# Both fixed passes of an expert stage from one dispatch, in a two-layer trunk kernel

## The chip, the core and the metric

The kernel runs on one core of one Trainium2 chip. The metric is the device time of one execution in microseconds. Engines are named as in the profile: PE is the matrix engine (TensorE) and PEld its weight loads, DVE the vector engine, ACT the scalar engine, POOL is GpSimd, and SP (SyncE) issues all transfers from DRAM in one queue. SBUF and PSUM are the on-chip memories; PSUM has eight banks, which the code calls bank(0) to bank(7).

## What is computed

The reference is a trunk of two layers over 512 tokens of width 1024, in float32. Layer 0 mixes tokens with an mLSTM of 4 heads, layer 1 with a short gated convolution; behind each stands a mixture of 32 experts, of which a token uses two. Before each sub-layer stands an RMSNorm with shift, scale and gate from a vector c. Cut to what matters:

```python
for i in range(DEPTH):                      # 2 layers
    h = rmsnorm(x, g) * (1.0 + scale) + shift
    y = mlstm_mixer(h, ...) if i == 0 else short_conv_mixer(h, ...)
    x = x + gate * y
    h = rmsnorm(x, g2) * (1.0 + scale2) + shift2
    # top group of 4, the top 2 of its 8 experts for each token, softmax weights
    out[t] = sum over t's two experts e of w * ((silu(h @ w_gate[e]) * (h @ w_up[e])) @ w_down[e])
    x = x + gate2 * out
return rmsnorm(x, final_g)
```

The mLSTM's head computes decayed scores of queries and keys over the causal triangle, their product with the values, and divides by a normaliser and by the root mean square of the result.

## The kernel before

The tokens lie in four tiles of 128 (TT = 4), a row of 1024 in eight blocks (KT = 8). The order of each engine's instructions is the order in which the program issues them; every engine works its queue in that order. A mixer is a list of steps in which products, small vector work and the adaLN vectors of later sub-layers (ada_third) are woven together by weave; how many of the latter stand where is set by FILL0 and FILL1.

**The ring.** Weights stream through tiles of 1 MB in pools L (2), A (8), B (8) and E (2). Ring.pump issues loads in one fixed order, and a load waits until its pool's oldest tile has been given back by done. The mixer borrows all eight B tiles (mixer_open): h and z in parts (own[0:4]), the split weights, scratch and a gate row. last_chunk gives the first of them back after two products and the second after four, open_ring all eight at the end of the mixer.

**An expert stage.** The 32 experts are worked in 13 passes of two or three experts, each pass with 128 slots for tokens. Passes 0 and 1 (FIXED = 2) hold known experts, so that their weights can be loaded before the routing is known. In a pass, dispatch gathers the tokens of its slots by products with a 0/1 matrix, up_project makes gate and up products, activate applies SiLU on ACT and multiplies on DVE, transposes and down follow, weigh and combine (called by finish in the next pass) add the result to xs. From pass 2 on the rows are dispatched from three bf16 parts (xp).

**The route** (tokens_here, tokens_done, route) overlaps the mixer's last product: for each token tile, rms, transposes (route_T), the normalised row in f32 (route_norm, ACT, line 1229), router logits and the selection (pick, some 14 small DVE steps). place computes the slots of the four fixed experts and hits the 0/1 matrix of pass 0 (line 1498); dispatch_0 gathers in f32 products of 128 columns (line 1524), first token tiles 0 and 1, then 2 and 3. dispatched (line 1530, ACT) applies scale and shift. Pass 1 gets its own matrix in arrange and its own dispatch_0 in pass 0, between activate and transposes and behind settle. route_parts and route_others split the rows in three bf16 parts on ACT, POOL and DVE during pass 0.

**A head of the mLSTM** is a list of steps: decay, four scores (one for each block of keys, all through bank 5, evacuated by DVE at line 867), four values, and heads_out (line 885), whose DVE part waits for POOL's power of -0.5 (line 900) and then scales the head's output (line 904).

Of the kernel before, what the change touches and what calls it, by code (L numbers as in the profile page):

```python
# [17 lines left out]
P = 128  # L18
# [5 lines left out]
H = 4  # L24
# [103 lines left out]
def trunk_kernel(  # L128
# [34 lines left out]
    def mixer_open(l):  # L163
# [4 lines left out]
        state["h"] = own[0:4]  # L168
        state["grow"] = own[7][:, 0:D]
        state["nml"], state["sT", 0] = own[6][0:H, 1536:], own[7][:, 1536:]  # L170
        state["m2"] = {"quart": [own[7][:, 1024 + 256 * i:1280 + 256 * i] for i in range(2)],
                       "tmp": [own[6][:, 512 * i:512 * i + 512] for i in range(3)],
                       "whi": [own[4][:, 512 * i:512 * i + 512].bitcast(F32R) for i in range(4)],
                       "wlo": [own[5][:, 512 * i:512 * i + 512].bitcast(F32R) for i in range(4)]}
# [209 lines left out]
    def ada_third(l, k, third):  # L384
# [262 lines left out]
    def last_chunk(ids, splits, banks, key, router, tokens_here, tokens_done):  # L647
# [3 lines left out]
        steps.extend(work[:2] + [Step(lambda: ring.take("B", 1))] + work[2:-1] + [Step(router)] + work[-1:])  # L651
        steps.append(Step(lambda: ring.take("B", 2)))
# [18 lines left out]
    def mlstm(fill, opened, router, tokens_here, tokens_done):  # L671
# [115 lines left out]
        def gates_4():  # L787
# [11 lines left out]
            m4 = state["sT", 0][0:H, :]  # L799
# [42 lines left out]
        def decay(h):  # L842
            def run():
# [3 lines left out]
                for s in range(2):  # L847
                    decays(h, s)
            return run

        def decays(h, s):
            w = state["m3"].tile([P, SEQ], F32, name="w", bufs=2)
            for t in range(s, TT):
                A.activation(out=w[:, (t - s) * P:(t - s + 1) * P], in_=state["pr"][:, t * P:(t + 1) * P],
                             func=AF.Exp, bias=state["bc"][:, s, t, h:h + 1])
            G.affine_select(out=w[:, 0:P], in_=w[:, 0:P], pattern=[[1, P]], compare_op=OP.is_ge, fill=0.0,
                            base=0, channel_multiplier=-1)
            state["w", s] = w

        def scores(h, s):  # L860
            def run():
                n = SEQ - s * P
                ps = bank(5)
                mm(ps[:, :n], lhsT=state["kT"][:, h, s * P:(s + 1) * P], rhs=state["qT"][:, h, s * P:],
                   start=True, stop=True)
                st = state["m3"].tile([P, n], F32, name="sT%d" % s) if s else state["sT", 0]
                V.scalar_tensor_tensor(out=st, in0=ps[:, :n], scalar=DK ** -0.5, in1=state["w", s][:, :n],
                                       op0=OP.mult, op1=OP.mult)
                state["sT", s] = st
                if s + 2 < TT:  # L870
                    decays(h, s + 2)
# [13 lines left out]
        def heads_out(h):  # L885
            def run():
                m1, num, o = state["m1"], state["num"], state["o"]
# [12 lines left out]
                G.tensor_tensor(out=sq, in0=sq, in1=mhalf, op=OP.pow)  # L900
                V.tensor_tensor(out=sq, in0=sq, in1=den, op=OP.mult)
# [15 lines left out]
        def head(h):  # L917
            return ([Step(decay(h))] + [Step(scores(h, s)) for s in range(TT)]
                    + [Step(values(h, t)) for t in range(TT)] + [Step(heads_out(h))])
# [70 lines left out]
        weave(c[4:], heads[0][0:1] + [Step(gates_5)] + heads[0][1:5], some(FILL0["v0b"]))  # L990
        weave(chunk("v1"), heads[0][5:] + heads[1][0:5], some(FILL0["v1"]))
# [901 lines left out]
```

## Time and profile before

| | |
|---|---|
| median of 3 runs | 1437.54 us (1437.41 to 1441.15) |
| the profiled execution | 1438.09 us, its span 1436.5 us |
| mean granted PE clock | 0.980 of full speed |
| busy | PE 1344.3 us (94%), DVE 646.4, ACT 399.8, POOL 90.9 |
| read from HBM | 489.57 MB, 342 GB/s over the span |

The span holds, in order, the mLSTM (to about 280 us), its expert stage (to about 745), the convolution (to about 955) and its expert stage. A busy PE in this profile includes time in which products wait in its pipe, so its 94% is an average over stages with different limits; the stages are read one by one.

### The profile page before, as it was taken

Reading aid. Unit: us, or ns where it says so; the run is one execution under the profiler, and the core shown is the slowest. Engines: PE = TensorE matmul, PEld = TensorE weight load, DVE = VectorE, ACT = ScalarE, POOL = GpSimd, SP = SyncE. Lnnn points to the kernel's source line nnn. Section 1 sums busy time; section 2 is a strip of 40 time slices with the busy share of each in tenths; the row PEclk is TensorE's granted clock in tenths of the full one; section 3 lists DMA queues with packets and bytes.
Section 4 is the critical chain, followed back from the end, with each engine's and each line's share of the span. In section 5 each row is a group of like instructions: output and inputs, shape, how many; then the busy total and the mean of one; then the engine's idle time right before and its main releaser. Section 6 shows DMA issues by size and latency. Waiting matters only on the chain. (4 is left out here: it accounts for less than half of the span.)

```text
span 1436.5 us, 24131 instructions
## 1 busy us (share of the span) xinstructions
PE 1344.3 (94%) x9693; PEld 795.1 (55%) x9694; DVE 646.4 (45%) x1353; ACT 399.8 (28%) x810; POOL 90.9 (6%) x94
## 2 busy tenths in 40 slices
PE   8999999999997699999899999999998599999997
PEld 6776777854442454444447787784443254444442
DVE  4497776564323022223247677757332303223224
ACT  4333445542110121112124333354111022111112
POOL 1022110020000000000003000102000000000000
PEclk9999999999999899999999999999999899999999
DMA  9977637669999999999997554867999999999995
GB/s 274 348 253 256 225 117 293 236 257 402 420 419 419 417 418 419 418 419 418 420 384 239 189 176 176 352 264 312 402 418 419 418 418 418 418 419 418 419 420 213
DMA packets 115341, 493.35 MB, mean 343 GB/s; under 512 B 14144, under 2 KB 43920, under 8 KB 66580
## 3 DMA queue, kind: packets, MB, share of 16 engines
q1 hardware_dynamic: 115220, 491.70, 86.8%
q8 instruction: 80, 1.31, 0.4%
q14 instruction: 41, 0.34, 0.1%
HBM read 489.57 MB, written 2.10 MB: 342 GB/s over the span
## 5 line engine op out<-in xcount | busy, mean ns | idle before, releaser
L1563 PE MATMUL b<-ringA,xT 128*32 128x512 f32 (+1 forms) x1248 | 189.1, 609 | 14.3 <-DMA ringA<-in_e_w_up_dram 10.4
L1563 PE MATMUL b<-ringB,xT 128*32 128x512 f32 (+1 forms) x1216 | 186.7, 595 | 9.9 <-DMA ringB<-in_e_w_up_dram 7.2
L1667 DVE TENSOR_TENSOR xs<-b,xs 128x512 f32<-128x512 f32 x204 | 126.7, 681 | 114.8 <-PE b L1666 114.7
L1514 PE MATMUL b<-P,xp 128*128 128x128 bf16 x2112 | 126.6, 223 | 22.7 <-PEq L1720 13.1
L1514 PEld LDWEIGHTS <-xp 128*128 128x128 bf16 x2112 | 124.2, 100 | 24.3 <-issue 24.1
L1654 DVE SCALAR_TENSOR_TENSOR sg<-b,ws,gate_row 128x512 f32<-128x512 f32 x26 | 19.5, 751 | 249.3 <-PE b L1590 238.1
L1563 PEld LDWEIGHTS b<-ringA,xT 128*32 128x32 f32 (+1 forms) x1248 | 51.0, 116 | 132.6 <-issue 94.5
L1563 PEld LDWEIGHTS b<-ringB,xT 128*32 128x32 f32 (+1 forms) x1216 | 53.9, 117 | 125.2 <-issue 98.3
L1573 DVE TENSOR_TENSOR act<-sg,b 128x512 f32<-128x512 f32 x26 | 27.9, 1075 | 192.0 <-issue 191.4
L1530 ACT ACTIVATE xT<-b,modcol 128x128 f32<-128x128 f32 x208 | 78.4, 458 | 128.8 <-PE b L1514 108.8
L499 ACT CAST ringB<-ringA 128x512 fp32r<-128x512 f32 (+1 forms) x132 | 77.3, 606 | 115.8 <-PE b L527 52.9
L500 DVE TENSOR_TENSOR ringB<-ringA,ringB 128x512 fp32r<-128x512 f32 (+1 forms) x128 | 89.7, 712 | 43.4 <-ACT ringB L499 43.3
L525 PE MATMUL b<-ringB 128*128 128x512 f32 x256 | 107.5, 420 | 0.0
L1583 ACT COPY actT<-b 128x512 f32<-128x512 f32 x26 | 15.3, 587 | 306.3 <-PE b L1581 306.3
L527 PE MATMUL b<-ringB 128*128 128x512 f32 x256 | 100.2, 391 | 0.0
L526 PE MATMUL b<-ringB 128*128 128x512 f32 x256 | 100.0, 391 | 0.0
L409 DVE SCALAR_TENSOR_TENSOR acc<-ringA,sc,acc 128x512 f32<-128x512 f32 x128 | 97.5, 785 | 4.9 <-DMA ringA<-in_s_w_in_dram 3.7
L1590 PE MATMUL b<-ringA,actT 128*32 128x512 f32 (+1 forms) x512 | 91.6, 606 | 5.3 <-DMA ringA<-in_e_w_down_dram 5.3
L1665 PE MATMUL b<-yh,pT 128*128 128x512 f32 x204 | 86.2, 422 | 1.8 <-ACT yh L1656 1.8
L1666 PE MATMUL b<-yl,pT 128*128 128x512 f32 x204 | 81.0, 397 | 0.7 <-DVE yl L1660 0.7
L544 PE MATMUL b<-m,ringB 128*128 128x512 f32 x192 | 75.5, 393 | 0.8 <-ACT m L458 0.8
L326 POOL TENSOR_TENSOR rstd<-rstd,mhalf 128x1 f32<-128x1 f32 x20 | 14.0, 703 | 972.7 <-DVE rstd L325 972.7
(339 smaller groups left out, 1873.7 us busy)
## 6 DMA issues: line engine op xcount, KB each, us to landing
ringB<-in_e_w_up_dram SPq DMA_DIRECT2D x84, 1024.0 KB, 19.8
ringA<-in_e_w_gate_dram SPq DMA_DIRECT2D x76, 1024.0 KB, 19.8
ringA<-in_e_w_down_dram SPq DMA_DIRECT2D x52, 1024.0 KB, 19.8
ringB<-in_e_w_down_dram SPq DMA_DIRECT2D x48, 1024.0 KB, 19.8
ringA<-in_ada_w_dram SPq DMA_DIRECT2D x40, 1024.0 KB, 5.0
ringA<-in_e_w_up_dram SPq DMA_DIRECT2D x40, 1024.0 KB, 19.8
ringB<-in_e_w_gate_dram SPq DMA_DIRECT2D x36, 1024.0 KB, 13.1
ringL<-in_e_w_down_dram SPq DMA_DIRECT2D x24, 1024.0 KB, 12.8
```

What stands on the lines that cost most here:

```text
L409: V.scalar_tensor_tensor(out=acc, in0=w, scalar=sc[:, j:j + 1], in1=acc, op0=OP.mult, op1=OP.add)
L500: on.tensor_tensor(out=to[1], in0=src, in1=to[0].bitcast(F32), op=OP.subtract)
L525: mm(ps, lhsT=lh, rhs=rh, start=first, stop=False)
L526: mm(ps, lhsT=lh, rhs=rl, start=False, stop=False)
L527: mm(ps, lhsT=ll, rhs=rh, start=False, stop=last)
L1514: mm(ps[:, q * P:(q + 1) * P], lhsT=S["xp"][i][:, t, j, :], rhs=flat[:, t, :], start=t == 0 and i == 0, stop=t == TT - 1 and i == 2)
L1530: A.activation(out=xT[:, j, :], in_=ps[:, q * P:(q + 1) * P], func=AF.Identity, scale=modcol[:, l, 1, 1, j:j + 1], bias=modcol[:, l, 1, 0, ...
L1563: mm(ps[c, :], lhsT=xT[:, k, c], rhs=weight(e, k), start=k == 0, stop=k == KT - 1)
L1590: mm(ps[half][c, :], lhsT=aT[:, j, c], rhs=weight(e, j, half), start=j == 0, stop=j == FT - 1)
L1665: mm(ps, lhsT=pT[:, t * P:(t + 1) * P], rhs=yh, start=True, stop=False)
L1666: mm(ps, lhsT=pT[:, t * P:(t + 1) * P], rhs=yl, start=False, stop=True)
L1667: V.tensor_tensor(out=xs[:, t, hs], in0=ps, in1=xs[:, t, hs], op=OP.add)
```

## The change

The gather of pass 0 and pass 1 becomes one: the rows are held as two f32r parts, high(t) (the row as rounded by ACT to f32r) and rest(t) (what is left, made by DVE in route_second), and one 0/1 matrix of 256 columns for four experts serves both passes. The products run over 4 token tiles, 2 parts and 8 blocks and gather in banks 0, 1, 2 and 6, where the half for pass 1 stays until pass 0's transposes. rest(t) lies in two B tiles, so the ring gets six B tiles at open_ring and the last two after the dispatch; no B tile is given back earlier. Since high(t) takes the place of the full row, route_parts makes the full rows again on ACT. settle uses bank 7 alone. The tiles sg and act become one (halves).

In the mLSTM the scores of key blocks 1 and 3 share one step, and the scaling of a head's output (heads_scaled) follows the next head's decay. Each gate row's two halves become two steps. In the last pass the second half's finish is split around the up products. The diff, cut:

```diff
-        state["h"] = own[0:4]
+        state["h"] = own[6:8] + own[0:2]
+        state["rows"] = own[6:8]
...
         if gate:
-            def rows_of():
-                row = state["grow"] if k == 0 else gate_row
-                for half in range(2):
+            def row_of(half):
+                def run():
+                    row = state["grow"] if k == 0 else gate_row
                     ps = bank(state["spare"])
                     mm(ps, lhsT=ones, rhs=mine["acc"][:, half * 512:(half + 1) * 512], start=True, stop=True)
                     A.copy(out=row[:, half * 512:(half + 1) * 512], in_=ps)
-            return Step(begin, after=True), work + [Step(rows_of)]
+                return run
+            return Step(begin, after=True), work + [Step(row_of(0)), Step(row_of(1))]
...
-        steps.extend(work[:2] + [Step(lambda: ring.take("B", 1))] + work[2:-1] + [Step(router)] + work[-1:])
-        steps.append(Step(lambda: ring.take("B", 2)))
+        steps.extend(work[:-1] + [Step(router)] + work[-1:])
...
+        PARTS = ({0: 0}, {1: 0, 3: 3 * P}, {2: 0})
...
+        def heads_scaled(h):
+            def run():
+                o, (num, den, sq) = state["o"], state["out"]
                 V.tensor_tensor(out=sq, in0=sq, in1=den, op=OP.mult)
                 for t in range(TT):
                     oh = o[:, t, h * DV:(h + 1) * DV]
...
+            late = [Step(heads_scaled(h - 1))] if h else []
+            return ([Step(decay(h))] + late + [Step(scores(h, part)) for part in PARTS],
+                    [Step(values(h, t)) for t in range(TT)] + [Step(heads_out(h))])
...
-            ring.take("B", RING["B"])
+            ring.take("B", RING["B"] - 2)
...
+        def row_of(t):
+            return xs[:, t, :].rearrange("p (q j) -> p j q", j=KT)
+
+        def high(t):
+
+            return normal(t).bitcast(F32R)
+
+        def rest(t):
+            return state["rows"][t // 2].rearrange("p (t j q) -> p t j q", t=2, j=KT)[:, t % 2].bitcast(F32R)
+
         def route_norm(t):
...
+            A.activation(out=high(t), in_=row_of(t), func=AF.Copy, scale=rstd[:, t:t + 1])
+
+        def route_second(t):
+            V.scalar_tensor_tensor(out=rest(t), in0=row_of(t), scalar=rstd[:, t:t + 1], in1=high(t).bitcast(F32),
+                                   op0=OP.mult, op1=OP.subtract)
 
         def route_parts():
...
+            S["xn"] = S["wk"].tile([P, TT, 2, KT, P], BF, name="xp12")
             S["xp"] = [S["wk3"].tile([P, TT, KT, P], BF, name="xp0"), S["xn"][:, :, 0], S["xn"][:, :, 1]]
+            for t in range(TT):
+                A.activation(out=normal(t), in_=row_of(t), func=AF.Copy, scale=rstd[:, t:t + 1])
             for t in range(TT):
                 A.copy(out=S["xp"][0][:, t], in_=normal(t))
...
                 pick((t - 2, PICK if t == 2 else 5))
+                route_second(t - 2)
...
+                S["hit"] = S["wk"].tile([P, TT, 2 * P], F32R, name="sg")
...
-            for half in range(2):
-                dispatch_0(range(2), half, held, S["hit"])
+            S["held"] = [bank(b) for b in (0, 1, 2, 6)]
+            dispatch_0([(t, part) for t in range(2) for part in range(2)])
             route_bias(last)
             pick((last, 5), (2, 5))
             pick((last, PICK - 5))
-            place(2, TT, before_in(2, TT))
+            pp = before_in(2, TT)
+            route_second(2)
+            place(2, TT, pp)
+            route_second(last)
+            dispatch_0([(2, 0), (2, 1), (last, 0)])
+            dispatch_0([(last, 1)])
             S["xT0"] = wk.tile([P, KT, P], F32, name="xT", bufs=1)
-            for half in range(2):
-                dispatch_0(range(2, TT), half, held, S["hit"])
-                dispatched(S["xT0"], half, held[half])
+            dispatched_0(S["xT0"], 0, range(KT))
+            ring.take("B", RING["B"])
             pick((0, 1), (1, 1), (2, 1), (last, 1))
-            A.copy(out=S["flat"], in_=S["hit"])
+            A.copy(out=S["flat"], in_=S["hit"][:, :, 0:P].bitcast(F32))
...
-            S["hit1"] = hits(PASSES[1], S["early"][:, :, 2:4], pt=wk.tile([P, TT, P], F32, name="pT", bufs=2))
...
-            pp = bank(6)
+            pp = bank(7)
             selb = S["all"]
             prefix(pp, selb)
-            pc = bank(7)
+            pc = pp[:, P:]
...
+        def dispatch_0(parts):
+
+            for j in range(KT):
+                for t, part in parts:
+                    mm(S["held"][j // 2][:, j % 2 * 2 * P:(j % 2 + 1) * 2 * P], lhsT=(rest if part else high)(t)[:, j, :],
+                       rhs=S["hit"][:, t, :], start=(t, part, j % 2) == (0, 0, 0), stop=(t, part, j % 2) == (TT - 1, 1, 1))
...
                 if last:
-                    finish(S["prev"], 1, (6, 7, None, None))
+                    finish(S["prev"], 1, (6, 7))
                 elif early:
                     finish(S["prev"], 0, (6, 7, None, None))
                 pu = up_project(cols, xT, 1, *weight(hu))
                 act = activate(pg, pu)
                 if p == 0:
                     weights()
-                    got = {}
-                    dispatch_0(range(TT), 0, got, S["hit1"])
-                if early and not last:
+                if last:
+                    finish(S["prev"], 1, (None, None), 2)
+                elif early:
                     finish(S["prev"], 1, (6, 7, None, None))
                 aT = transposes(act)
                 if p == 0:
                     S["xT"] = wk.tile([P, KT, P], F32, name="xT", bufs=1)
-                    dispatched(S["xT"], 0, got[0])
+                    dispatched_0(S["xT"], 1, (6, 7, 0, 1, 2, 3, 4, 5))
                     settle()
-                    dispatch_0(range(TT), 1, got, S["hit1"])
-                    dispatched(S["xT"], 1, got[1])
                     following()
```

## Rows read from the trace of the kernel before

**Rows 1.** The page: the transfer rate in 40 equal slices of the span (35.9 us each).

```profile
GB/s 274 348 253 256 225 117 293 236 257 402 420 419 419 417 418 419 418 419 418 420 384 239 189 176 176 352 264 312 402 418 419 418 418 418 418 419 418 419 420 213
```

**Rows 2.** Windows: each engine's busy time in a stretch, then the granted PE clock, the share of the DMA engines' time and the rate in GB/s. Three stretches of layer 0's expert stage and one of layer 1's.

```profile
296.00:300.00 4.00, 4.00 (x22) 1.33 (x20) 3.76 (x10) 3.03 (x5) 0.00 (x0) 1.00 0.34 82
...
316.00:320.00 4.00, 4.00 (x20) 1.30 (x20) 0.61 (x1) 4.00 (x10) 1.93 (x2) 1.00 0.03 8
...
700.00:720.00 20.00, 20.00 (x208) 10.96 (x202) 6.48 (x11) 5.32 (x12) 0.00 (x0) 0.99 1.01 417
...
988.00:992.00 4.00, 4.00 (x23) 1.74 (x23) 0.69 (x1) 3.23 (x8) 1.09 (x1) 1.00 0.23 90
```

**Rows 3.** The timeline of SyncE's queue in layer 0: start, us from the first to the last of the merged instructions, what is loaded, how many.

```profile
319.49 4.69 SPq L89 DMA_DIRECT2D ringA<-in_e_w_gate_dram  x4
```

**Rows 4.** The timeline of DVE around the route: start, us, line, operation, shapes; in brackets the idle time before it and what ended that. The last row is the same step in layer 1.

```profile
276.29 0.19 DVE L1324 TENSOR_TENSOR xh<-xh,actT 128x32 f32<-128x32 f32 x1
277.78 0.69 DVE L586 TENSOR_TENSOR ringB<-b,ringB 128x512 f32<-128x512 f32 x1 [1.30 <-PE b L527]
...
283.05 0.17 DVE L1352 SCALAR_TENSOR_TENSOR early<-b,selb 128x8 f32<-128x8 f32 x1 [0.62 <-PE b L1411]
283.25 0.42 DVE L1498 TENSOR_TENSOR sg<-slots,early 128x256 f32<-128x256 bf16 x1
...
286.53 0.35 DVE L1405 TENSOR_TENSOR selb<-selb 128x4 bf16<-128x4 bf16 x2
...
289.36 0.17 DVE L1352 SCALAR_TENSOR_TENSOR early<-b,selb 128x8 f32<-128x8 f32 x1 [2.49 <-PE b L1411]
...
957.52 0.17 DVE L1352 SCALAR_TENSOR_TENSOR early<-b,selb 128x8 f32<-128x8 f32 x1 [0.61 <-PE b L1411]
```

**Rows 5.** The timeline of PE over the same stretch: two f32r products of the mixer, the two halves of the dispatch of pass 0 (32 records for 16 products each), the first gate products; the last row is the start of the gate in layer 1.

```profile
277.11 0.40 PE L526 MATMUL b<-ringB 128*128 128x512 f32 x1
277.35 0.39 PE L527 MATMUL b<-ringB 128*128 128x512 f32 x1
...
283.82 5.44 PE L1524 MATMUL b<-sg,xp 128*128 128x128 f32 x32 [0.85 <-DVE sg L1498]
...
290.04 3.84 PE L1524 MATMUL b<-sg,xp 128*128 128x128 f32 x32 [0.76 <-DVE sg L1498]
...
293.90 3.65 PE L1563 MATMUL b<-ringL,xT 128*64 128x512 f32 x16
...
966.75 0.65 PE L1563 MATMUL b<-ringL,xT 128*64 128x512 f32 x2
```

**Rows 6.** The timeline of ACT in pass 0 of layer 0: four of the eight scale-and-shift steps, the copy of the 0/1 matrix, the last of the small activations, the four casts of route_parts, the SiLU.

```profile
292.19 1.51 ACT L1530 ACTIVATE xT<-b,modcol 128x128 f32<-128x128 f32 x4 [8.75 <-PE b L1524]
...
295.31 0.63 ACT L1372 CAST P<-sg 128x512 bf16<-128x512 f32 x1
...
298.85 0.20 ACT L1396 ACTIVATE t_sl<-t_gm 128x4 f32<-128x4 f32 x1
301.04 3.88 ACT L1239 CAST xp<-xp 128x1024 bf16<-128x1024 f32 x4 [1.98 <-PE b L1563]
304.83 0.59 ACT L1571 ACTIVATE sg<-b 128x512 f32<-128x512 f32 x1
```

**Rows 7.** Groups of instructions by line and form over the whole span: line, engine, operation, shapes, count; busy us and mean ns of one; idle time before them.

```profile
L1573 DVE TENSOR_TENSOR act<-sg,b 128x512 f32<-128x512 f32 x26 | 27.9, 1075 | 192.0 <-issue 191.4 <-PE b L1563 0.6
...
L1654 DVE SCALAR_TENSOR_TENSOR sg<-b,ws,gate_row 128x512 f32<-128x512 f32 x26 | 19.5, 751 | 249.3 <-PE b L1590 238.1 <-PE b L1622 11.2
...
L1229 ACT ACTIVATE xp<-xs,rstd 128x1024 f32<-128x1024 f32 x8 | 17.5, 2191 | 0.0
```

**Rows 8.** The timeline of all engines in pass 0 of layer 0, from the end of the up products to the down products: the first half of pass 1's dispatch, the product of SiLU and up, the second half, settle's last step, the down products.

```profile
307.79 3.84 PE L1524 MATMUL b<-pT,xp 128*128 128x128 f32 x32
...
308.00 1.08 DVE L1573 TENSOR_TENSOR act<-sg,b 128x512 f32<-128x512 f32 x1 [0.30 <-PE b L1563]
...
312.06 3.82 PE L1524 MATMUL b<-pT,xp 128*128 128x128 f32 x32
...
312.42 0.17 DVE L1456 TENSOR_TENSOR key<-b,room 1x32 f32<-1x32 f32 x1
...
315.81 7.09 PE L1590 MATMUL b<-ringA,actT 128*64 128x512 f32 x32
```

**Rows 9.** The timeline of PE where the expert stage of layer 0 tests for leftover tokens: the two longest gaps, in brackets.

```profile
471.62 0.69 PE L1514 MATMUL b<-P,xp 128*128 128x128 bf16 x5 [6.38 <-PEq L1720]
477.12 6.07 PE L1514 MATMUL b<-P,xp 128*128 128x128 bf16 x65 [4.81 <-issue]
```

**Rows 10.** Windows behind those gaps; the third number from the end is the granted PE clock.

```profile
480.00:481.50 1.50, 1.50 (x17) 1.50 (x16) 0.00 (x0) 0.00 (x0) 0.00 (x0) 0.50 1.06 431
482.00:485.00 3.00, 3.00 (x59) 2.98 (x61) 0.00 (x0) 1.80 (x5) 0.00 (x0) 1.00 0.99 410
```

**Rows 11.** Groups of PE products and one row of waits: the scores in the mLSTM (62 to 262 us), the gate rows over the whole span, and DVE's waits for POOL's power in the mLSTM (us in total, times, longest).

```profile
L864 PE MATMUL b<-qT,kT 128*128 128x512 f32 (+3 forms) x32 | 11.9, 452 | 3.9 <-DVE sT L867 2.8 <-DVE ringB L867 1.1
...
L420 PE MATMUL b<-acc,ones 128*128 128x512 f32 x16 | 8.7, 628 | 3.1 <-ACT ringB L421 1.4 <-ACT gate_row L421 1.4 <-DVE acc L409 0.4
...
DVE sq L901 <- POOL sq L900: 4.8, 4, 1.2
```

**Rows 12.** The timeline of PE in the last pass of layer 1, at the transposes.

```profile
1411.66 0.66 PE L1581 MATMUL b<-ident,act 128*128 128x128 f32 x4 [1.21 <-DVE act L1573]
```

More of the change, by code (lines that the diff above doesn't have):

```diff
@@ L861, in run, with scores @@
+            state["w", min(part)] = w
+        def scores(h, part):
             def run():
-                n = SEQ - s * P
                 ps = bank(5)
[L864 to L867, printed above, removed]
+                first = min(part)
+                n = sum(SEQ - s * P for s in part)
+                for s, at in part.items():
+                    mm(ps[:, at:at + SEQ - s * P], lhsT=state["kT"][:, h, s * P:(s + 1) * P],
+                       rhs=state["qT"][:, h, s * P:], start=True, stop=True)
+                st = state["m3"].tile([P, n], F32, name="sT%d" % first) if first else state["sT0"]
+                V.scalar_tensor_tensor(out=st, in0=ps[:, :n], scalar=DK ** -0.5, in1=state["w", first][:, :n],
@@ L868, in run @@
                                        op0=OP.mult, op1=OP.mult)
[L869 to L871 removed]
+                for s, at in part.items():
+                    state["sT", s] = st[:, at:at + SEQ - s * P]
+                if first == 0:
+                    decays(h, PARTS[2])
             return run
@@ L1516, in dispatch, with dispatched_0 @@
             return ps
[L1518 to L1525 removed]
+        def dispatch_0(parts):
[3 more added lines that the diff above has]
+                       rhs=S["hit"][:, t, :], start=(t, part, j % 2) == (0, 0, 0), stop=(t, part, j % 2) == (TT - 1, 1, 1))
+        def dispatched_0(xT, p, js):
+            for j in js:
+                at = j % 2 * 2 * P + p * P
+                A.activation(out=xT[:, j, :], in_=S["held"][j // 2][:, at:at + P], func=AF.Identity,
+                             scale=modcol[:, l, 1, 1, j:j + 1], bias=modcol[:, l, 1, 0, j:j + 1])
         def dispatched(xT, half, ps):
@@ L1566, in up_project, with halves @@
             return ps
+        def halves():
+            both = S["wk"].tile([P, 2, 512], F32, name="sg")
+            return [both[:, i] for i in range(2)]
         def activate(pg, pu):
-            wk = S["wk"]
-            sg = wk.tile([P, FF], F32, name="sg")
+            sg, act = (part.rearrange("s (q j) -> s q j", j=P) for part in halves())
+            sg = sg.rearrange("s q j -> s (q j)")
             A.activation(out=sg, in_=pg, func=AF.Silu)
-            act = wk.tile([P, FT, P], F32, name="act")
             V.tensor_tensor(out=act, in0=sg.rearrange("s (q j) -> s j q", j=FT),
@@ L1728, in count, with finish @@
                                   max_val=most, skip_runtime_bounds_check_because="a count of tokens bounds it")
-        def finish(prev, half, banks):
+        def finish(prev, half, banks, first=0):
             pT, yh, yl = prev
-            for t, b in enumerate(banks):
+            for t, b in enumerate(banks, first):
                 combine(pT, yh[half], yl[half], t, half, psA() if b is None else bank(b))
@@ L1816, in run @@
                 yh, yl = parts()
-                yf = [wk.tile([P, 512], F32, name=n) for n in ("sg", "act")]
+                yf = halves()
                 if last:
```

83 lines of the change are left out of this document (36 added, 47 removed).

## The prediction

> **What bounds the kernel now.** I read the page first, for the transfer rate by slices [rows 1]: two long plateaus at about 418 GB/s (slices 10 to 20 and 29 to 39) are the two expert stages, and between them lie the mixers, where the rate is low and TensorE (PE) is nearly always busy. Windows then show how each plateau begins [rows 2]. In layer 0 the DMA engines are nearly idle at 296-300 (share 0.34) and 316-320 (0.03); layer 1 has the same hole at 988-992 (0.23). Later the share stays at 1.01, to the pass at 700-720. The ring is why: SyncE's queue issues the next four loads at 319.49 [rows 3], when the down products of pass 0 give ring tiles back. So up to then the PE's order of work sets the clock, and afterwards bytes do: a pass-0 down stage that begins d us later moves everything behind it by d, since the plateau has no slack to win it back, and one that begins earlier is a gain until the holes are closed. The question is thus one for each layer: when does the down stage of pass 0 begin (315.81 in layer 0 [rows 8])? The mixers count in full as well, since they come before it.
>
> **The route up to the first gate product.** The PE work does not shrink here. Of the old dispatch, 32 PE records (two for each of 16 products of 128 f32 columns) take 3.84 us, 0.120 each [rows 5]. The new one needs 64 products of 256 columns in f32r, each with one load of 128 weight columns. The trace has no f32r product of 256 columns; the nearest row is that record, with a weight load of the same form, so I take 0.120 (64 x 0.120 = 7.7 us, as now). The upper end is the f32 price by column, 0.24 per 128, so 0.48 each; the lower end half of the 0.24 between an L526 and the next L527, f32r products of 512 columns [rows 5], so the two nearest rows agree.
>
> What is added is DVE work: route_second, four passes of 128x1024 with one input read in steps of 8 floats. No such DVE pass is in the trace. Contiguous, the 0.75 us of L1654 for 512 elements [rows 7] and the 0.25 us between L1498's 256 elements (0.42) and the 0.67 I take for 512 give about 1.3 us for 1024. L1573, read with strides, takes 1.08 for 512, so about 2.0, and ACT's L1229, which reads the very same view, 2.19 [rows 7]. I take 2.1 (call it r), nearest to the row with the same view; the ends are 1.3 and 2.3. The Trainium skill ("SBUF — State Buffer", section "Door 1: The DMA port swizzle") says that consecutive accesses within a 16-byte line run at full rate and each step to a new line pays; with 32-byte steps every element does, which speaks against this change, and L1573 and L1229 agree. Read without that penalty the sum below would be at its lower end.
>
> Two of the four passes stand in the last chunk, in front of a token tile's output on the DVE queue: behind them wait L586 and L587, which finish xs, and for xs the PE's transposes. In front of the last L586 DVE idles 1.30 us (L1324 ends 276.48, L586 starts 277.78 [rows 4]), so xs of tile 3 comes 2r - 1.3 = 2.9 us later, and so does L1352 (283.05, then 285.95). From there DVE needs 3.82 us to the end of L1405 (286.88), 0.25 more for hits of twice the width, then r for the third pass; then 0.95 to the finished hits (0.68 now), 24 products (2.9), 8 more behind the fourth pass (which is hidden by the 24: 2.1 against 2.9), and 0.2 for the count. The gate begins at 285.95 + 3.82 + 0.25 + 2.1 + 0.95 + 2.9 + 0.96 + 0.2 = 297.1, against 293.90 [rows 5]: **+3.2**. Layer 1 has the same chain from 957.52 [rows 4], 971.6 against 966.75: **+4.85**. (In layer 0 the first half of the old dispatch took 5.44 instead of 3.84, which hides 1.6.)
>
> **Pass 0.** Removed are both halves of pass 1's dispatch, 3.84 + 3.82 = 7.66 us of PE between the up products and the down products [rows 8]. But high() overwrites the full rows with rounded ones, so route_parts makes them again on ACT: four more passes of L1229's kind, 8.76 us, and ACT is a queue. Behind them stand the four casts of L1239 and then the SiLU that activate needs. Today the casts end at 304.92 and the SiLU starts at 304.83 [rows 6], before the up products end (307.8), so ACT costs nothing; that cover goes. From the gate's start: the eight L1530 begin 0.9 earlier (as soon as the first columns are complete) and take 3.0 (1.51 for 4), so +2.1; from L1372 to the end of L1396 3.74, so +5.9; the rows 8.76, +14.6; casts 3.88, +18.5; SiLU 0.59, +19.1; L1573 1.08, +20.2; transposes and the copy 1.25, +21.5; two L1530 that free bank 6, +22.3. Bank 7 is now settle's and is given back only after weights() and L1456 on DVE: L1573's start to L1456's end is 4.6 us now (308.00 to 312.59 [rows 8]), of which 0.3 waits for PE, so +23.4; two down products can go before. The down stage begins at about +23.1 instead of 315.81 - 293.90 = +21.9: **+1.2**, where -7.66 is meant. PE stands still from +13.9 to +20.2, 6.3 us.
>
> A gap like that has a price. After 6.38 us without work (to 471.62) and 4.81 more (to 477.12) [rows 9] the granted clock was 0.5, still at 480-481.5 with work since 477.12, and 1.0 again at 482-485 [rows 10]. Half speed for some 4.5 us of the down stage costs **+2.2** (bounds 0 and 3.4).
>
> So d = 3.2 + 1.2 + 2.2 = 6.6 in layer 0 and 4.85 + 1.2 + 2.2 = 8.25 in layer 1: **+14.85**.
>
> **What gains.** In the mLSTM the PE waits 3.9 us for a score's evacuation out of one bank [rows 11]; three steps for a head instead of four, and a DVE queue that no longer stands 4.8 us at POOL's power [rows 11], should take **-3** (bounds 0 and -3.9). The two halves of a gate row in steps of their own remove four waits of 0.7 us (1.4 + 1.4 [rows 11]): **-2.6** (0 to -2.8). In each layer's last pass four of the eight combine products move into the 1.21 us in which PE waits for act [rows 12]; at about 0.24 each (L526 to L527): **-1.9** for both (0 to -1.9). Sum -7.5.
>
> **At nothing:** the first two B loads move from the last chunk to behind the dispatch. In SyncE's queue the L loads stand behind them. Their 2 MB take 5 us and fit into the hole at 296-300 and the longer one before the down stage; without it they would cost 5 us in each layer. hits share a tile with the router's weights and wait for the last logits, but the prefix product they need stands behind those logits on the PE anyway. The later rests on POOL are needed only in pass 1's own dispatch.
>
> **Sum.** 1438.1 (the profiled execution) + 14.85 - 7.5 = 1445.4; the median of the runs is 0.55 under the profiled one, so **1445 us**.
>
> **Rivals.** (1) *The removed products decide, faster.* If ACT wrote a row in 1.0 us (as a contiguous L1239 cast) instead of 2.19, its chain would be 4.8 shorter: down begins 3.8 earlier than now after the gate, no clock is lost, and with r = 1.3 by the same cause (gate +0.8 and +2.4) d is -3.0 and -1.4: 1438.1 - 4.4 - 7.5 - 0.5 = **1426**. It decides below some 1.3 us a row. Against it: all eight L1229 took about 2.19. Chance 0.13. (2) *A wash.* The chain on ACT holds, but DVE reads strided rows at the contiguous rate and the clock does not fall: d = 0.8 + 1.2 and 2.4 + 1.2, sum 5.6 - 7.5: about **1436**. Against it: both strided rows of [rows 7]; for it, that L1573 reads two strided inputs and the new pass only one. Chance 0.22. (3) *256 columns do not run at the f32r rate.* At 0.48 each, 64 products take 30.7 instead of 7.7; with some 5 of it beside DVE's passes that is +18 in each layer: about **1480**. Chance 0.04. (4) *It does not do what it says:* the two dispatches still stand apart. The code has one accumulation of 256 columns, so nothing is left for this.
>
> **How the numbers follow.** Forecast 0.61. Its bounds: r = 1.3 to 2.3, clock 0 to 3.4, gains of 3 to 7.5 give about 1436 to 1452. The range takes in the wash, 1434 to 1452, and leaves out (1) and (3). A measurement of this kernel tells about 0.3% (4.3 us) from no change. Slower by over that (above 1441.8): nearly all of the forecast and (3), 0.62; within: the rest of the forecast and most of (2), 0.23; faster: (1) and a little of (2), 0.15.
>
> **What would show it.** Profile after: L586 of the last tile waits behind a DVE pass of about 2.1 us; PE idle near 6 us between up products and transposes in pass 0, ended by ACT through DVE's act; the SiLU after eight ACT passes over 128x1024; granted clock 0.5 in the down stage; down at gate +23. The hole in the DMA share before the down stage grows from about 4 to 10 us. Wrong if the SiLU does not wait for the rows, if route_second takes about 1.3, or if the mLSTM gives more than its visible waits.

## The result: slower by 1.2%, and where the time went

The changed kernel takes **1457.51 us** (median of 4 runs, 1454.87 to 1459.53), the kernel before 1439.35 in the same comparison (1437.41 to 1441.84): ratio 1.0124, 95% interval 1.0097 to 1.0151. The forecast had the side right and the size wrong: 1445 in a range of 1434 to 1452. The profiled executions have spans of 1456.9 and 1436.5, 20.4 apart, some 2 us more than the medians.

That difference splits by stages. Each cell is a distance between first starts of lines in PE's timeline: the router step (the first product with the router's weights), the first gate product of pass 0, the first gate product of pass 1, the transposes of the last pass. The last two rows are kernels of the next section.

| us | to layer 0's router step | router to gate | gate to pass 1 | pass 1 to last transposes | layer 1: to its router step | router to gate | gate to pass 1 | pass 1 to last transposes | to the end |
|---|---|---|---|---|---|---|---|---|---|
| before | 256.15 | 37.75 | 29.66 | 414.86 | 192.19 | 36.14 | 29.66 | 415.25 | 24.84 |
| after | 257.47 | 44.56 | 32.61 | 415.18 | 191.87 | 42.88 | 32.66 | 414.87 | 24.80 |
| difference | +1.32 | **+6.81** | **+2.95** | +0.32 | -0.32 | **+6.74** | **+3.00** | -0.38 | -0.04 |
| e2_fill | 257.89 | 40.29 | 29.63 | 415.14 | 191.72 | 40.63 | 29.65 | 415.23 | 24.82 |
| e10_final | 257.45 | 39.06 | 25.10 | 416.12 | 191.71 | 39.11 | 25.11 | 415.39 | 24.85 |

So 19.5 of the 20.4 us lie in the route and in pass 0, in both layers alike. Nothing was won in the mixers or at the end. The +1.32 of layer 0's mixer can't be read from one profile: seven kernels below have the very same mixer, and their router steps lie between 255.51 and 258.12.

The route after, on DVE (layer 0): the new passes, the last tile's output, the places. Compare [rows 4].

```profile
273.90 2.10 DVE L1257 SCALAR_TENSOR_TENSOR ringB<-xs,rstd,xp 128x1024 fp32r<-128x1024 f32 x1
...
279.51 2.07 DVE L1257 SCALAR_TENSOR_TENSOR ringB<-xs,rstd,xp 128x1024 fp32r<-128x1024 f32 x1
281.51 0.67 DVE L588 TENSOR_TENSOR ringB<-b,ringB 128x512 f32<-128x512 f32 x1
282.21 0.69 DVE L589 TENSOR_TENSOR xs<-xs,ringB 128x512 f32<-128x512 f32 x1
...
289.54 0.17 DVE L1384 SCALAR_TENSOR_TENSOR early<-b,selb 128x8 f32<-128x8 f32 x1 [3.89 <-PE b L1450]
...
296.96 0.17 DVE L1384 SCALAR_TENSOR_TENSOR early<-b,selb 128x8 f32<-128x8 f32 x1 [1.25 <-PE b L1450]
```

The same on PE: transposes and logits of the last tile, then the two parts of the dispatch and the gate. Compare [rows 5].

```profile
283.05 1.94 PE L1239 MATMUL b<-ident,xs 128*128 128x128 f32 x8 [2.05 <-DVE xs L589]
...
285.86 3.58 PE L1307 MATMUL b<-sg,pT 128*128 128x36 f32 x16
...
290.48 0.58 PE L1558 MATMUL b<-sg,xp 128*128 128x256 f32 x1 [1.02 <-DVE sg L1388]
...
294.06 0.41 PE L1558 MATMUL b<-sg,xp 128*128 128x256 f32 x1
294.28 0.41 PE L1558 MATMUL b<-sg,ringB 128*128 128x256 f32 x1
...
295.73 0.28 PE L1558 MATMUL b<-sg,xp 128*128 128x256 f32 x1
295.85 0.28 PE L1558 MATMUL b<-sg,ringB 128*128 128x256 f32 x1
...
302.03 2.37 PE L1603 MATMUL b<-ringL,xT 128*64 128x512 f32 x10
```

Windows of the same kernel: busy time of each engine, granted clock, DMA share, GB/s. The first three lie in the route, the last two in pass 0.

```profile
286.00:289.50 3.50, 3.46 (x19) 3.38 (x18) 0.00 (x0) 1.74 (x1) 0.00 (x0) 0.50 1.01 424
290.50:295.50 5.00, 5.00 (x23) 5.00 (x24) 4.83 (x22) 0.00 (x0) 0.00 (x0) 0.50 0.64 269
298.00:301.80 3.80, 3.80 (x32) 3.79 (x32) 3.08 (x7) 0.42 (x2) 0.00 (x0) 1.00 0.70 257
324.00:329.80 5.80, 5.75 (x14) 1.72 (x16) 3.54 (x9) 5.19 (x12) 3.07 (x3) 0.50 0.01 4
330.50:334.00 3.50, 3.50 (x20) 0.96 (x17) 3.36 (x4) 1.16 (x2) 1.63 (x2) 1.00 0.64 208
```

Read the three together. The pass of 2.07 us stands straight in front of L588, as forecast. PE has nothing to do for 2.05 us, and behind that wait the granted clock is 0.5, the lower of the two levels (1.2 GHz). The logits of the last tile then take 3.58 us, the dispatch products follow each other by 0.213 us; as soon as the clock is 1.0 again (295.73) they follow by 0.120.

Pass 0 after, on ACT and PE. Compare [rows 6, 8].

```profile
307.80 8.33 ACT L1268 ACTIVATE xp<-xs,rstd 128x1024 f32<-128x1024 f32 x4
316.05 3.87 ACT L1270 CAST xp<-xp 128x1024 bf16<-128x1024 f32 x4
319.82 0.58 ACT L1615 ACTIVATE sg<-b 128x512 f32<-128x512 f32 x1
```

```profile
312.81 3.17 PE L1603 MATMUL b<-ringA,xT 128*64 128x512 f32 x14
321.55 1.12 PE L1624 MATMUL b<-ident,sg 128*128 128x128 f32 x4 [5.56 <-DVE sg L1616]
...
324.05 9.92 PE L1633 MATMUL b<-ringA,actT 128*64 128x512 f32 x32 [1.12 <-ACT xT L1564]
```

The SiLU (L1615) stands behind eight ACT passes and is done 4.4 us after the up products (end 315.98); PE waits 5.56 us, and the down stage takes 9.92 instead of 7.09 at clock 0.50. DMA is idle in 324.00:329.80 (share 0.01), a hole some 7 us long where it was about 4 [rows 2].

### The profile page after: what moved, and what is told of

Read it like the earlier page. It is cut to its first block, busy times and chain, and to the rows that moved or that the text cites. A ratio compares the mean times of both kernels' runs of the same rounds, so it can differ in the third digit from the quotient of the medians.

```text
span 1456.9 us, 23857 instructions
## 1 busy us (share of the span) xinstructions
PE 1350.9 (93%) x9565; PEld 792.2 (54%) x9566; DVE 654.0 (45%) x1355; ACT 416.5 (29%) x818; POOL 86.6 (6%) x94
## 5 line engine op out<-in xcount | busy, mean ns | idle before, releaser
L1697 DVE SCALAR_TENSOR_TENSOR sg<-b,ws,gate_row 128x512 f32<-128x512 f32 x52 | 38.9, 751 | 250.4 <-PE b L1633 239.5
L1616 DVE TENSOR_TENSOR sg<-sg,b 128x512 f32<-128x512 f32 x26 | 27.8, 1070 | 214.9 <-PE b L1603 176.6
L1633 PE MATMUL b<-ringA,actT 128*32 128x512 f32 (+1 forms) x512 | 97.4, 633 | 7.5 <-DMA ringA<-in_e_w_down_dram 5.3
L1626 ACT COPY actT<-b 128x512 f32<-128x512 f32 x26 | 15.2, 586 | 302.0 <-PE b L1624 302.0
L1570 ACT ACTIVATE xT<-b,modcol 128x128 f32<-128x128 f32 x176 | 66.1, 456 | 103.3 <-PE b L1550 103.3
L1699 ACT CAST yh<-sg 128x512 fp32r<-128x512 f32 x52 | 32.1, 619 | 156.5 <-DVE sg L1697 156.4
```

What stands on the lines that cost most here:

```text
L1633: mm(ps[half][c, :], lhsT=aT[:, j, c], rhs=weight(e, j, half), start=j == 0, stop=j == FT - 1)
```

## The experiments

All kernels ran beside the kernel before on the same chip; a ratio is to that kernel, with its 95% interval.

**The mixer's part alone (e1_heads).** On the kernel before:

```diff
+ PARTS = ({0: 0}, {1: 0, 3: 3 * P}, {2: 0})     # three score steps
+ late = [Step(heads_scaled(h - 1))] if h else []
- return ..., work + [Step(rows_of)]
+ return ..., work + [Step(row_of(0)), Step(row_of(1))]
+ finish(S["prev"], 1, (None, None), 2)           # last pass, behind activate
```

> The kernel before with only the mixer's part of the change: three score steps for a head, the scaling of a head's output behind the next head's decay, a gate row in two steps, and the last pass's finish split in two. The dispatch, its rows and the ring stay as before. The sum of the prediction gives -7.5 us (1432). Theory after the first comparison (layer 0's mixer +1.3, layer 1's -0.3, last passes 0 in the changed kernel): the waits that this removes were covered, and other waits take their place, so 1438 to 1440, no change. A rival: the new order of a head costs by itself, 1441 to 1443, and then layer 0's mixer ends 1 us or more later than before (router's step after 256.15).

Measured: 1438.09 against 1437.82, ratio 1.0002 (0.9993 to 1.0011). The forecast gain of 7.5 us isn't there. The view of PE's waits from 20 to 258 us (us in total, times, longest) shows why; compare [rows 11]:

```profile
PE b L871 <- DVE ringB L874: 1.6, 1, 1.6
PE b L846 <- DVE ringB L802: 1.2, 1, 1.2
...
PE b L526 <- DVE xn L831: 0.7, 1, 0.7
```

The waits of the scores fell from 3.9 to 1.6 us and those of the gate rows are gone, but PE now waits 1.2 us for DVE's scan (L802) ahead of head 0's decay and 0.7 at a projection product (L526) for DVE's copy of the values (L831). In this profile the router step stands 2 us later than before, at 258.19, as the rival had it; but the same mixer gave 255.51 to 258.12 elsewhere, and the time did not move. Two more runs asked whether that is the new place of a step or DVE's pace.

**One empty step (e9_heads_pad)** and **gate rows in one step (e11_heads_one)**, both on e1_heads:

```diff
  weave(c[4:], heads[0][0][:1] + [Step(gates_5)] + heads[0][0][1:]
+       + [Step(lambda: None)], ...)                       # e9
- work + [Step(row_of(0)), Step(row_of(1))]                # e11
+ work + [Step(rows_of)]
```

> As the first run (the kernel before with the mixer's part of the change alone), with one empty step added at the end of head 0's list in the second half of chunk v0, so that this list has six entries again and its steps stand at the same places among the projection's products as before. No work is added. Theory 'spacing': with three score steps the list had five entries, the decay came one place earlier among the products, and TensorE waited 1.25 us there for DVE's scan and then ran at half clock for 3.4 us; with six entries that wait goes and layer 0's mixer is 2 to 3 us shorter than in the first run: 1435.5. Rival: the next wait takes its place (DVE's queue is the same length), no change, 1438.

> The kernel before with the three score steps and the late scaling of a head's output (and the last pass's finish split), but a gate row made in one step as before. Theory 'shift': the second step of each gate row moves every later step of the modulation by one place against the projections, and that is what put DVE's scan behind other work and TensorE's new 1.25 us wait ahead of head 0's decay; without it that wait and the half clock after it are gone, the score waits stay shorter, and the kernel gains about 2 to 3 us: 1435.5. The gate rows' four waits of 0.7 us are back. Rival: the mixer is paced by DVE's queue as a whole (80% busy from 60 to 200 us), so the sum of TensorE's waits stays near 6.5 to 7 us wherever they stand: 1438.

Measured: e9 1439.55, 1.0004 (0.9993 to 1.0014); e11 1438.70, 1.0000 (0.9991 to 1.0009). Neither theory's 2 to 3 us came, and both rivals (no change) hold. In e9 the decay's wait is still 1.2 us and one of 0.9 has come at a score. In e11 it is gone, as "shift" said, but others are there:

```profile
PE b L870 <- DVE ringB L873: 2.7, 2, 2.3
PE b L887 <- DVE modcol L349: 1.0, 1, 1.0
...
PE b L420 <- ACT ringB L421: 0.7, 1, 0.7
PE b L420 <- ACT gate_row L421: 0.7, 1, 0.7
```

So the gate rows' second step did move the scan, and that explains nothing of the time. Three orders of the mixer give three sets of waits and one time: in layer 0 PE's waits from 20 to 258 us add up to 6.3 us in e1, 7.6 in e9 and 7.1 in e11, against 7.2 before. That DVE's queue paces it agrees with all three; it was not shown by taking work from DVE there.

**The clock (e2_fill).** Idle products in PE's waits, nothing moved:

```diff
+ busy(bank(5)[:, 0:P], 28)    # ahead of route_T(last)
+ busy(bank(4)[:, 0:P], 14)    # ahead of each half of the dispatch
+ busy(bank(3)[:, 0:P], 85)    # pass 0, ahead of transposes
```

> The changed kernel with idle products (bf16, 128 columns, results unused) put where TensorE waits: 28 ahead of the last tile's transposes in the route, 14 ahead of each half of the first dispatch, 85 ahead of pass 0's transposes. No work is moved. Theory 'clock': the half clock that follows these waits is on the path; with the granted clock held at 1.0 the last logits go from 3.58 back to 2.0 us and the first 32 dispatch products from 6.4 to 3.9, so the gate comes 3.3 us earlier in layer 0 and 1.8 in layer 1, and the pass-0 down stage goes from 9.95 to 7.1 in both: 1457.5 - 10.8 = 1446.7. Rival 'queues': DVE's and ACT's passes set these times alone and the clock lies beside them: 1455 to 1458.

Measured: 1446.26, 1.0056 (1.0041 to 1.0072), within 0.5 us of the theory. PE's timeline:

```profile
281.25 1.73 PE L322 MATMUL b<-onesb 128*128 128x128 bf16 x28
283.49 1.13 PE L1239 MATMUL b<-ident,xs 128*128 128x128 f32 x8 [0.50 <-DVE xs L589]
...
285.01 1.93 PE L1307 MATMUL b<-sg,pT 128*128 128x36 f32 x16
...
298.18 1.08 PE L1606 MATMUL b<-ringL,xT 128*64 128x512 f32 x4
```

xs of the last tile comes as late as in the changed kernel (the transposes at router +25.60, there +25.58), but the logits take 1.93 instead of 3.58, and the granted clock is 1.00 all through the route (280 to 298). The gate comes 4.27 us earlier than in the changed kernel in layer 0 and 2.25 in layer 1, and pass 0 is 2.98 and 3.01 shorter. Work that computes nothing bought some 11 us: 11.25 by the two medians, which come from different comparisons, and about 10 by the two ratios.

**Where the stride stands (e3_natural).** The rounded rows and remainders in the row's own order:

```diff
- A.activation(out=high(t), in_=row_of(t), ...)
+ A.activation(out=high(t), in_=xs[:, t, :], ...)          # likewise in route_second
- lhsT=(rest if part else high)(t)[:, j, :]
+ lhsT=(rest if part else high)(t).rearrange("p (q j) -> p j q", j=KT)[:, j, :]
```

> The changed kernel, but the rounded rows and their remainders lie in the order of the row itself, so that ACT's and DVE's four passes each read and write side by side; the dispatch's weight loads take every eighth element instead. Theory: the 32-byte step is what makes the passes 2.14 and 2.19 us; they become about 1.3 (DVE) and 1.0 to 1.1 (ACT), the last tile's output waits 1.7 us less, the 2.05 us wait of TensorE ahead of its transposes goes to under 0.5, the clock doesn't fall there, and the gate comes some 4.5 us earlier in layer 0 and 3.5 in layer 1: 1449.5. Rival (a): the passes keep 2.1, the step is not their price: 1457. Rival (b): a weight load with a step costs more than it hides (0.1 us more for each of 64 in a layer, +6 a layer): 1461 to 1470.

Measured: 1459.13, 1.0147 (1.0131 to 1.0162). The theory's number missed by 10 us, and rival (b)'s lies a little above the measured one; the profile shows both mechanisms. Groups of instructions (busy us, mean ns of one, idle before), then PE's timeline; the granted clock is 1.00 from 281.5 to 285.3 and from 290 to 291, and 0.50 from 288 to 289:

```profile
L1257 DVE SCALAR_TENSOR_TENSOR ringB<-xs,rstd,xp 128x1024 fp32r<-128x1024 f32 x8 | 10.2, 1278 | 0.0
L1254 ACT ACTIVATE xp<-xs,rstd 128x1024 fp32r<-128x1024 f32 x8 | 9.3, 1163 | 0.0
```

```profile
281.73 1.13 PE L1239 MATMUL b<-ident,xs 128*128 128x128 f32 x8 [0.33 <-DVE xs L589]
...
283.25 1.93 PE L1307 MATMUL b<-sg,pT 128*128 128x36 f32 x16
...
288.56 0.44 PE L1558 MATMUL b<-sg,ringB 128*128 128x256 f32 x1
288.80 0.44 PE L1558 MATMUL b<-sg,xp 128*128 128x256 f32 x1
...
290.19 0.41 PE L1558 MATMUL b<-sg,xp 128*128 128x256 f32 x1
290.43 0.41 PE L1558 MATMUL b<-sg,ringB 128*128 128x256 f32 x1
```

Side by side, DVE's pass takes 1.28 us and ACT's 1.16; PE's wait falls from 2.05 to 0.33 and the logits keep the full clock, as they did in e2, where the wait was filled. But a product whose weights are taken with a step of eight elements follows the one before by 0.24 us, at the full and at the half clock alike, where the changed kernel has 0.12 and 0.213, and 128 products pay that. The Trainium skill ("SBUF — State Buffer", section "Door 1: The DMA port swizzle") lets each access that crosses to a new 16-byte line pay, and both engines' passes agree: DVE's 2.14 with the step and 1.28 without, ACT's 2.19 and 1.16. The Trainium skill ("TensorE: Matmul & The Clock Gate", section "LDWEIGHTS (loading the stationary operand)") prices a weight load by its columns alone; by that this form would cost as much as the other, which the 0.24 speaks against, and the measurement decides.

**Full rows in a spare tile (e5_act).** ACT writes the full row with the step, then casts it; DVE subtracts side by side (tiles 0 to 2):

```diff
+ A.activation(out=full, in_=row_of(t)[:, js], func=AF.Copy, scale=rstd[:, t:t + 1])
+ A.copy(out=high(t)[:, js], in_=full)
+ V.tensor_tensor(out=rest(t)[:, js], in0=full, in1=high(t)[:, js].bitcast(F32), op=OP.subtract)
```

> The changed kernel, but for tiles 0 to 2 ACT first writes the full row column-ordered into a spare tile (two halves, read with the step as now), then casts it to the rounded row side by side, so that DVE's remainder is a difference of two tiles that lie side by side (two passes of 128x512); tile 3 as now. The dispatch's weight loads are as in the changed kernel. Theory: DVE's pass falls from 2.14 to about 1.4 us and the weight loads keep 0.12, so TensorE's wait ahead of the last transposes goes from 2.05 to under 0.6, the clock stays at 1.0 through the logits, and the gate comes at router +37.5 to 38 in both layers (+44.56 and +42.88 now): 1457.5 - 11.5 = 1446. Rival: ACT, with 3.4 us a tile instead of 2.19 in its queue, holds up the copies of the transposed tile and the squares of the next, and the gate comes no earlier than +41: 1452 or more.

Measured: 1462.63, 1.0166 (1.0150 to 1.0181). The rival was right, and for a second reason: with one spare tile ACT waits for DVE's subtraction of the tile before.

```profile
274.48 1.35 ACT L1260 ACTIVATE ringB<-xs,rstd 128x512 f32<-128x512 f32 x1 [2.61 <-DVE ringB L1267]
...
278.20 0.62 ACT L317 ACTIVATE ringB<-xs 128x512 f32<-128x512 f32 x1
```

The squares of tile 2 (L317) come behind both halves, DVE waits 2.63 us for them, and the gate comes at router +45.7 and +46.3.

**Who makes the rows again (e4_shared).** Two of the four on DVE, two casts behind the SiLU:

```diff
- for t in range(TT): A.activation(out=normal(t), in_=row_of(t), ...)
+ for t in range(2): A.activation(out=normal(t), in_=row_of(t), ...)
+ for t in range(2, TT): V.tensor_scalar(out=normal(t), in0=row_of(t), scalar1=rstd[:, t:t + 1], ...)
...
+ route_casts()                  # the casts of tiles 2 and 3, behind activate
```

> The changed kernel, but of the four full rows that are made again in pass 0 two are made on DVE, which idles 8.14 us there, and the casts of these two come behind the SiLU in ACT's queue. Theory: the SiLU waits for ACT's eight passes alone, so it starts right after the up products (gate+14 instead of +17.8), TensorE's wait ahead of the transposes falls from 5.56 to about 1.7 us, the clock stays at 1.0 and the down stage takes 7.1 instead of 9.95: pass 0 (gate to gate) goes from 32.6 to about 26.7 in both layers, 1457.5 - 12 = 1445.5. Rival: the banks (settle's behind DVE, the eight copies of the second pass's columns on ACT) hold the down stage at gate+21 to +22 anyway; then only the clock may come back, 1451 to 1457.

Measured: 1443.47, 1.0044 (1.0027 to 1.0062). By the medians that is 2 us better than the theory; by the two ratios the gain is 11.5 us, against 12. PE's timeline, then a window of the down stage:

```profile
313.02 0.66 PE L1630 MATMUL b<-ident,sg 128*128 128x128 f32 x4 [1.27 <-DVE sg L1622]
...
315.06 8.81 PE L1639 MATMUL b<-ringA,actT 128*64 128x512 f32 x32 [1.23 <-ACT xT L1570]
```

```profile
315.10:318.30 3.20, 3.20 (x8) 0.84 (x10) 3.06 (x10) 3.20 (x9) 0.55 (x1) 0.50 1.00 422
```

Pass 0 takes 26.7 from gate to gate in both layers instead of 32.6. Here the removed products pay: 3 us less than before the change, though the route still loses. One part of the theory failed: the clock did fall, and the down stage takes 8.81 us, not 7.1.

The run shows something else. Its route is that of the changed kernel, line for line, and PE waits the same 2.05 us in it (layer 0). But the clock is back sooner, the last logits take 2.12 us instead of 3.58, and the gate comes at router +42.30 in both layers. So the +44.56 and +42.88 of the table hold for one profile, and the price of the clock in the route differs between profiles.

**Repairs together (e6_both, e8_shared_fill, e7_mix, e10_final, e12_final_one).** e6 is e4 and e5 with weights() ahead of activate and fillers; e8 is e4 with the fillers of the route and two short ones in pass 0; e7 is e8 with e5's form for tiles 1 and 3 only, place(2, TT) ahead of the remainders of tiles 2 and 3, 14 instead of 28 idle products ahead of the last transposes, and another order in the second half of the dispatch; e10 is e7 with settle's prefix in bank 5 and the empty step of e9; e12 is e10 without that step and with gate rows in one.

```diff
- pp = bank(7)                  # settle, e10 and e12
+ pp = bank(5)
- if t == TT - 1: ...           # e7: full rows for odd tiles only
+ if t % 2 == 0: ...
```

> The changed kernel with the two repairs together (two of the remade rows on DVE with their casts behind the SiLU; remainders as differences of side-by-side tiles), the combine weights of DVE ahead of the SiLU's product, and three short fillers of idle bf16 products (13, 13, 18) in TensorE's waits of about 1 us ahead of each dispatch half and of pass 0's transposes. Theory: the gate is back near its old place (router +37.5 against +37.75 and +36.14 before) and pass 0 from gate to gate takes 24.5 to 25.5 instead of 29.66, at full clock, since 7.66 us of dispatch are really gone: 1438 + 1.2 - 9 = 1430, below the kernel before. Rival 'the plateau': an earlier pass 0 gives nothing back later because the loads of the second ring half, moved behind the dispatch, then end later than the products want them: 1436 to 1440.

> The changed kernel with the shared remade rows and the fillers alone (28 ahead of the last transposes in the route, 14 and 14 ahead of the dispatch halves, 18 and 18 in pass 0); the remainders as in the changed kernel. Theory: stages add. Gate at router +40.3 and +40.6 (as with the fillers alone) against +37.75 and +36.14 before, pass 0 at 25.0 from gate to gate against 29.66: 1438.5 + 2.5 + 4.5 - 9.3 = 1436. Rival: the two repairs overlap (the fillers' gain in the down stage was already in the shared rows), so 1439 to 1442.

> The changed kernel with: two of the remade rows on DVE and their casts behind the SiLU (as in the run that did this alone); for tiles 1 and 3 only, ACT writes the full row first and DVE's remainder is a difference of side-by-side tiles; the places of tiles 2 and 3 ahead of the remainders of tiles 2 and 3 in DVE's queue; short fillers of idle bf16 products in TensorE's waits (14, 14, 14, 18, 18). Theory: the spare tile is now free when ACT wants it, so the last tile's output is only some 1.2 us late, DVE's last remainder ends at router +37, the gate comes at +38 to +38.5 in both layers, and pass 0 takes 24.9 from gate to gate: 1438.5 + 0.5 + 2.1 - 9.6 = 1431.5. Rival: ACT's 3.7 us for a tile again hold up the squares of the next one and the gate stays at +41 or later: 1437 or more.

> The version with both repairs (the one with tiles 1 and 3 by ACT's full row) plus the empty step of the other run of this pair, and the prefix product of pass 0's settling in bank 5 instead of bank 7, so that the down products no longer wait 0.72 us for DVE to read bank 7. Theory: the down stage takes 7.1 instead of 8.03 us in both layers (-1.9) and the mixer gives the 2 to 3 us of the other run: 1436.3 - 1.9 - 2.3 = 1432. Rival: only the bank counts, 1434.5.

> The last repaired version (full rows for tiles 1 and 3, shared remade rows, fillers, bank 5) without the empty step and with a gate row in one step. Theory 'shift': 2 to 3 us less than the 1435.7 of that version, 1433. Rival: no difference, 1435.5.

| | median us | ratio | interval |
|---|---|---|---|
| e6_both | 1461.07 | 1.0154 | 1.0140 to 1.0169 |
| e8_shared_fill | 1437.44 | 0.9994 | 0.9985 to 1.0004 |
| e7_mix | 1436.32 | 0.9985 | 0.9976 to 0.9993 |
| e10_final | 1435.68 | 0.9982 | 0.9973 to 0.9991 |
| e12_final_one | 1437.16 | 0.9987 | 0.9978 to 0.9996 |

e6 missed by 31 us. Its route is e5's, and pass 0 lost what e4 had won (transposes at gate +19.6 instead of +15.2): weights() now stands on DVE ahead of the SiLU's product and takes 5.2 us there (314.40 to 319.58). Some 2.3 us of that are three small steps that took longer than in the changed kernel; they ran beside POOL's rests (L1310 on POOL, 312.21 to 317.75).

```profile
314.69 0.85 DVE L1536 TENSOR_SCALAR t_at<-t_ex 128x4 f32<-128x4 f32 x1
...
315.79 0.86 DVE L1538 TENSOR_TENSOR t_at<-t_at,t_gi 128x4 f32<-128x4 f32 x1
316.68 1.07 DVE L1539 TENSOR_TENSOR t_at<-t_at,t_ex 128x4 f32<-128x4 f32 x1
```

In the changed kernel these three took 0.14, 0.16 and 0.17 (L1516, L1518, L1519). That POOL slowed them was not tested, and three other small steps beside the same passes (a reduction and two reciprocals, L1534, L1535, L1537) took 0.17 and 0.18. e8 came within 1.5 us of its theory, though its pass 0 takes 26.05 us, not 25.0. e7 and e10 missed theirs by 4.8 and 3.7: the gate comes at +39.1, not +38 to +38.5, e7's pass 0 takes 26.04, not 24.9, and the mixer's 2 to 3 us don't exist. The bank's part held, since in e10 the down stage takes 7.09 us, so e10's rival (only the bank counts, 1434.5) was the nearer one:

```profile
313.86 7.09 PE L1654 MATMUL b<-ringA,actT 128*64 128x512 f32 x32 [0.22 <-ACT xT L1585]
```

e10 is faster than the kernel before by some 2.6 us, 0.18%: its two passes 0 are 4.56 and 4.55 us shorter, its routes 1.31 and 2.97 longer. e12, whose interval overlaps e10's, shows no gain from the order in the mixer.

## Why the prediction was wrong, point by point

- **The frame** was right: from pass 1's gate to the last transposes it is 415.2 and 414.9 after, 414.9 and 415.3 before. A later pass 0 moves all behind it, and the B loads, moved past the dispatch in SyncE's queue, cost nothing there.
- **The sizes of the new passes** were right: DVE's remainder takes 2.14 us (2.1 taken), a product of 256 columns in f32r 0.120 at full clock (0.120 taken), ACT's row 2.15 (2.19 taken).
- **The route is the first step that failed.** The sum was "+3.2" and "+4.85", made of DVE's passes at full clock; it measured +6.81 and +6.74. DVE's part, read from e2_fill, where the clock holds, is +2.54 and +4.49. The other 6.5 us (3.7 in e4's profile of the same route) are the half clock behind PE's waits in the route, the longest of which the prediction itself had made ("xs of tile 3 comes 2r - 1.3 = 2.9 us later"). It priced half speed in pass 0 and gave the route none, though the logits and 64 products follow there.
- **Pass 0** had nearly the right size, +2.95 and +3.00 against 1.2 + 2.2, but in part by luck, since two errors cancel. The down stage begins at gate +22.0, not +23.1 (the rows took 8.33, not 8.76, and the chain behind the SiLU was shorter), so the queues cost 0.1, not 1.2; and the half clock costs 2.8 to 2.9, not 2.2 (the upper end was 3.4). e4 and e2 show both causes.
- **The gains are the second step that failed.** "-3", "-2.6" and "-1.9" added up waits of PE that the change removes; e1_heads measures the three together as 0 (interval -1.0 to +1.6 us). Their lower bound of nothing was named, but the sum took nearly all, and the range was drawn with 3 to 7.5. In the mixer other waits of PE came in place of those removed; why is argued above and not shown. In the last pass the removed wait came back as transfer time: the act wait of [rows 12] is gone, and the up products, which begin earlier against their loads, take 8.26 us for 32 instead of the 7.09 of before. e1_heads has the same (8.25 us, with a wait of 0.98 for the load). The prediction's own frame had said that bytes set the time in this stage. PEld's timeline of layer 1 names what the products wait for; then PE's shows the stage, and last the same products in the kernel before:

```profile
1427.23 0.20 PEld L1603 LDWEIGHTS b<-ringB,xT 128*64 128x64 f32 x4 [0.99 <-DMA ringB<-in_e_w_up_dram]
```

```profile
1422.62 8.26 PE L1603 MATMUL b<-ringB,xT 128*64 128x512 f32 x32
...
1432.10 0.66 PE L1624 MATMUL b<-ident,sg 128*128 128x128 f32 x4
```

```profile
1403.36 7.09 PE L1563 MATMUL b<-ringB,xT 128*64 128x512 f32 x32
```

- **The rivals.** (1) did not happen, but its mechanism is real: where the rows don't hold up the SiLU, pass 0 falls to 25.1 us (e10_final) from 29.66. (2) fell with both of its conditions, DVE's rate and the clock; (3) fell with the 0.120, and (4) with the one dispatch of 256 columns in the trace.
- **The sum.** Forecast for the profile +7.35. Then -1.0 (DVE's part in the route), +6.5 (the clock there), -0.85 (pass 0), +7.5 (gains), and +0.9 in the other cells of the table, of which +1.3 is within the spread of layer 0's mixer: +20.4.

## What to carry to other kernels

Price a wait of PE twice, once for its length and once for the products behind it at half clock, at every place where the change makes one and not only at the longest. How long the clock then stays low can't be read off the wait: behind the same 2.05 us the logits took 3.58 us in one profile and 2.12 in another. A wait that an edit removes is no gain where other work or the transfers hold the stage anyway: here 7.5 us of waits were counted as gains and nothing was won, which a run of that edit alone showed. The strided access was paid by whoever made it: moving the step from DVE and ACT to the weight loads moved the cost to 128 products.

## What the runs showed of the hardware that was not expected

A weight load of 128 f32r columns taken every eighth element doubles the time from product to product, 0.24 against 0.12 us, at the full clock; at half the clock it is 0.24 as well, against 0.213. Three small DVE steps of 0.14 to 0.17 us took 0.85 to 1.07 beside POOL's tensor passes, while three others beside the same passes took 0.17 and 0.18. A DVE scale of 128x1024 with the step takes 1.62 us where the two-input form takes 2.16 (L1270 and L1257 of e4_shared, means of 4 and 8). And the same route in layer 0 took 37.75 us to the gate in the profile of the kernel before, with a stretch of half clock in it, and 36.12 in that of e11_heads_one, without; the changed route took 44.56 in one profile and 42.30 in another.
